# Instance normalisation over 512 channels: from 32 units of 16 channels to 22 units of 16 or 24

## The chip, the cores and the metric

The kernel runs on one core of one Trainium2 chip. The metric is the device time in microseconds (us); the time before is the median of three runs. Engines are called PE (TensorE, matrix products), DVE (VectorE), ACT (ScalarE), POOL (GpSimd) and SP (SyncE, which here only issues transfers). SP, ACT and POOL each have a queue on which they issue transfers (DMA) between the chip's main memory and the on-chip memory of 128 partitions; all queues feed the core's 16 DMA engines.

## What is computed

```python
def setup_inputs():
    B, G, C_per_g, H, W = 4, 8, 16, 256, 256
    return {
        "x": np.random.randn(B, G, C_per_g, H, W).astype(np.float32),
        "gamma": np.random.randn(G, C_per_g).astype(np.float32),
    }

def reference(x, gamma):
    B, G, C_per_g, H, W = x.shape
    mu = x.mean(axis=(3, 4), keepdims=True)
    var = ((x - mu) ** 2).mean(axis=(3, 4), keepdims=True)
    x_norm = (x - mu) / np.sqrt(var + 1e-5)
    out = x_norm * gamma[None, :, :, None, None]
    return out.astype(np.float32)
```

There are 4 x 8 x 16 = 512 channels of 65,536 fp32 values, 256 KB each: 134.2 MB are read and 134.2 MB are written. Each channel is brought to mean 0 and variance 1 and multiplied by its gamma. A channel must be read whole before any of it can be written.

## The kernel before

The input is cut into 32 units of 16 channels, 4 MB each. A channel lies on 8 partitions of a tile of 128 x 8,192 values, so a row of a partition is 32 KB, contiguous in main memory. Six such tiles, the slots `xt0` to `xt5`, take 192 KB of each partition. Unit u lives in slot u mod 6.

The order of the work is written out by hand (the schedule is manual; waits are set by what reads and writes the same tile). Before the loop, POOL issues a small store (`touch`, 16 pieces of 512 bytes of the first output unit, overwritten later) and the load of gamma; then the loads of units 0 to 5 are issued, 1 and 3 on ACT's queue and the others on SP's. POOL builds a mask `navg` of 128 x 128 that holds -1/65536 where two partitions belong to the same channel. Gamma is spread to one value a partition by eight small products of PE (`g_col`, one column for each of the eight units after which gamma repeats).

For each unit, in this order:

- DVE sums each row (`st`, L106), and beside it ACT squares each row and sums the squares (L107; the squares themselves go to `junk`).
- PE multiplies `navg` with the two sums (L115): each partition then has minus its channel's mean and minus its mean square in `ps`.
- DVE makes minus the variance (L116), ACT the root (L120), DVE its reciprocal (L124) and the scale with gamma (L126).
- DVE applies both in one pass over the tile, in place (L135). In unit 0 alone ACT does the last three eighths (L132, with a `shift` that DVE makes, L131).
- ACT issues the store (L139), and SP the load of unit u + 6 into the same slot (L48), which waits for the store to have landed.

Of the kernel before, what the change touches and what calls it, by code (L numbers as in the profile page):

```python
# [1 line left out]

# [4 lines left out]

F32 = mybir.dt.float32
U8 = mybir.dt.uint8
ALU = mybir.AluOpType  # L10
ACTF = mybir.ActivationFunctionType
AX = mybir.AxisListType


@with_exitstack
def kernel(
    ctx: ExitStack,
    tc: tile.TileContext,
    x: bass.AP,
    gamma: bass.AP,  # L20
    out: bass.AP,
):
    nc = tc.nc
    B, G, C, H, W = x.shape
    P = nc.NUM_PARTITIONS
    HW = H * W
    n_ch = B * G * C
    S = 8
    K = P // S
    F = HW // S  # L30
    U = n_ch // K
    NG = (G * C) // K
    AHEAD = 6
    assert HW % S == 0 and (G * C) % K == 0

    xv = x.rearrange("b g c h w -> (b g c h w)").rearrange("(u p f) -> u p f", p=P, f=F)
    ov = out.rearrange("b g c h w -> (b g c h w)").rearrange("(u p f) -> u p f", p=P, f=F)
    gv = gamma.rearrange("g c -> (g c)")

    data = ctx.enter_context(tc.tile_pool(name="data", bufs=1))  # L40
    singles = ctx.enter_context(tc.tile_pool(name="singles", bufs=1))
    psum = ctx.enter_context(tc.tile_pool(name="psum", bufs=4, space=bass.MemoryType.PSUM))
    ctx.enter_context(tc.manual_schedule())

    slots = [data.tile([P, F], F32, name=f"xt{i}") for i in range(AHEAD)]

    def load(u, queue):
        queue.dma_start(out=slots[u % AHEAD][:], in_=xv[u])  # L48


    g_row = singles.tile([1, G * C], F32, name="g_row")
    touch = singles.tile([16, 128], F32, name="touch")
    nc.vector.memset(touch[:], 0.0)  # L53
    nc.gpsimd.dma_start(out=ov[0][0::S, 0:128], in_=touch[:])  # L54
    nc.gpsimd.dma_start(out=g_row[:], in_=gv[None, :])  # L55
    for u in range(AHEAD):
        load(u, nc.scalar if u in (1, 3) else nc.sync)

    eps_t = singles.tile([P, 1], F32, name="eps_t")
    nc.gpsimd.memset(eps_t[:], 1e-5)  # L60
    one = singles.tile([1, 1], F32, name="one")
    nc.gpsimd.memset(one[:], 1.0)
    navg = singles.tile([P, K, S], F32, name="navg")
    nc.gpsimd.memset(navg[:], -1.0 / HW)  # L64
    nc.gpsimd.affine_select(  # L65
        out=navg[:], in_=navg[:], pattern=[[-S, K], [0, S]], compare_op=ALU.is_ge,
        fill=0.0, base=0, channel_multiplier=1,
    )
    nc.gpsimd.affine_select(  # L69
        out=navg[:], in_=navg[:], pattern=[[S, K], [0, S]], compare_op=ALU.is_ge,  # L70
        fill=0.0, base=S - 1, channel_multiplier=-1,
    )
    navg_w = navg[:].rearrange("p k s -> p (k s)")
    root_eps = singles.tile([P, 1], F32, name="root_eps")
    nc.scalar.activation(out=root_eps[:], in_=eps_t[:], func=ACTF.Sqrt)  # L75
    g_rep = singles.tile([1, NG, K, S], F32, name="g_rep")
    g_ps = psum.tile([P, NG], F32, name="g_ps", bufs=1)
    g_col = singles.tile([P, NG], F32, name="g_col")

    nc.vector.tensor_copy(  # L80
        out=g_rep[:],
        in_=g_row[:].rearrange("o (n k) -> o n k", n=NG).unsqueeze(3).to_broadcast([1, NG, K, S]),
    )
    for n in range(NG):
        nc.tensor.matmul(  # L85
            out=g_ps[:, n : n + 1],
            lhsT=g_rep[:, n].rearrange("o k s -> o (k s)"),
            rhs=one[:],
            start=True, stop=True,
        )  # L90
    nc.vector.tensor_copy(out=g_col[:], in_=g_ps[:])  # L91

    junk = singles.tile([P, F], U8, name="junk")

    st = singles.tile([P, U, 2], F32, name="st")
    nvar = singles.tile([P, U], F32, name="nvar")
    std = singles.tile([P, U], F32, name="std")
    rstd = singles.tile([P, U], F32, name="rstd")
    scale = singles.tile([P, U], F32, name="scale")

    shift = singles.tile([P, 1], F32, name="shift")

    squares = []
    for u in range(U):
        t = slots[u % AHEAD]
        nc.vector.reduce_sum(out=st[:, u, 0:1], in_=t[:], axis=AX.X)  # L106
        square = nc.scalar.activation(  # L107
            out=junk[:], in_=t[:], func=ACTF.Square, accum_out=st[:, u, 1:2],
        )
        if u:  # L110

            tc.declare_no_dep(square.ins, squares[-1].ins, reason="junk, ordered by the root between")
        squares.append(square)
        ps = psum.tile([P, 2], F32, name="ps")
        nc.tensor.matmul(out=ps[:], lhsT=navg_w, rhs=st[:, u], start=True, stop=True)  # L115
        nc.vector.tensor_scalar(  # L116
            out=nvar[:, u : u + 1], in0=ps[:, 0:1], scalar1=ps[:, 0:1],
            scalar2=ps[:, 1:2], op0=ALU.mult, op1=ALU.add,
        )
        nc.scalar.activation(  # L120
            out=std[:, u : u + 1], in_=nvar[:, u : u + 1], func=ACTF.Sqrt,
            bias=eps_t[:], scale=-1.0,
        )
        nc.vector.reciprocal(out=rstd[:, u : u + 1], in_=std[:, u : u + 1])  # L124
        g = u % NG
        nc.vector.tensor_mul(  # L126
            out=scale[:, u : u + 1], in0=rstd[:, u : u + 1], in1=g_col[:, g : g + 1],
        )
        cut = F * 5 // 8 if u == 0 else F
        if cut < F:  # L130
            nc.vector.tensor_mul(out=shift[:], in0=ps[:, 0:1], in1=scale[:, u : u + 1])  # L131
            nc.scalar.activation(  # L132
                out=t[:, cut:], in_=t[:, cut:], func=ACTF.Identity, bias=shift[:], scale=scale[:, u : u + 1],
            )
        nc.vector.tensor_scalar(  # L135
            out=t[:, :cut], in0=t[:, :cut], scalar1=ps[:, 0:1], scalar2=scale[:, u : u + 1],
            op0=ALU.add, op1=ALU.mult,
        )
        nc.scalar.dma_start(out=ov[u], in_=t[:])  # L139
        if u + AHEAD < U:  # L140
            load(u + AHEAD, nc.sync)


# [1 line left out]
_INS = ['x', 'gamma']  # L145
_OUTS = [((4, 8, 16, 256, 256), 'float32')]


# [23 lines left out]
```

## Time and profile before

| What | us |
|---|---|
| Time before, median of three runs (627.28 to 627.58) | 627.53 |
| Span of the profiled execution, first to last instruction | 625.2 |
| Time before less that span | 2.3 |
| DVE busy | 441.8 |
| ACT busy | 241.8 |
| One sum of 128 x 8,192 on DVE (L106) | 8.68 |
| One square of 128 x 8,192 on ACT (L107) | 7.03 |
| One apply of 128 x 8,192 on DVE (L135) | 4.55 |
| Store, issue to landing, median | 62.5 |
| Load on SP's queue, issue to landing, median | 38.5 |

The profile is of one execution, and durations are read from it. The runs' times are taken without the profiler: the 2.3 us are the difference of that median and this span, and no time of the profiled execution itself is given beyond its span. In the page, rows of slices cut the span in 40 equal parts; busy shares are in tenths and GB/s is what the DMA engines moved. A group's line gives the line of the kernel, engine, operation, tiles and shapes, the count, the busy time and the mean of one in ns, and the idle time ahead with what ended it. A window's line gives the busy time of each engine between two times of the span.

### The profile page before, as it was taken

What the parts mean: (1) busy time and instruction counts of PE and PEld (TensorE: products, weight loads), DVE (VectorE), ACT (ScalarE), POOL (GpSimd) and SP (SyncE); (2) the same over time, 40 slices, a digit from 0 to 9 for tenths busy, and PEclk for the clock granted to TensorE, in tenths of its full rate; (3) what the DMA queues carried; (4) which work ended last, traced back from release to release, by engine and by line L of the source; (5) the groups of instructions that cost most, each with busy time, mean ns of one, the idle gap of its engine ahead of it and who ended that gap; (6) DMA issues with size and microseconds to landing.
All of it is one profiled execution on the core that took longest, in us unless ns stands there. A gap on an engine that the chain in (4) does not pass through costs nothing.

```text
span 625.2 us, 635 instructions
## 1 busy us (share of the span) xinstructions
PE 21.4 (3%) x80; PEld 19.5 (3%) x80; DVE 441.8 (71%) x164; ACT 241.8 (39%) x99; POOL 2.4 (0%) x11
## 2 busy tenths in 40 slices
PE   0200000000000000000000000000000000000000
PEld 0200000000000000000000000000000000000000
DVE  0589999998776687666786767867668676687730
ACT  0464444444443244432344423444224442244400
POOL 1000000000000000000000000000000000000000
DMA  8999999999999999999999999999999999999998
GB/s 370 436 407 432 436 436 436 436 436 430 423 436 434 434 428 434 434 436 436 436 436 428 426 436 436 432 430 434 434 436 436 436 436 421 432 436 434 434 430 367
DMA packets 9282, 268.46 MB, mean 429 GB/s; under 512 B 1072, under 2 KB 1088, under 8 KB 1088
## 3 DMA queue, kind: packets, MB, share of 16 engines
q10 hardware_dynamic: 4896, 142.61, 52.9%
q1 hardware_dynamic: 4320, 125.83, 46.8%
q0 software_dynamic: 64, 0.01, 0.0%
q14 instruction: 2, 0.02, 0.0%
HBM read 134.22 MB, written 134.23 MB: 429 GB/s over the span
## 4 chain that ended last, share of the span: by engine, by line
another core or an unknown queue 61%; DMA 17%; DVE 15%; SPq 1%; PE 1%; issue 0%; ACT 0%
DMA xt<-in_x_dram 10%; DVE st L106 10%; DMA out_dram<-xt 8%; DVE xt L135 5%; SPq L48 1%; PE ps L115 1%; ACT std L120 0%; DVE nvar L116 0%; DVE rstd L124 0%; DVE scale L126 0%; DVE shift L131 0%
## 5 line engine op out<-in xcount | busy, mean ns | idle before, releaser
L106 DVE TENSOR_REDUCE st<-xt 128x1 f32<-128x8192 f32 x32 | 277.9, 8684 | 102.2 <-DMA xt<-in_x_dram 102.2
L107 ACT ACTIVATE junk<-xt 128x8192 uint8<-128x8192 f32 x32 | 225.0, 7030 | 272.0 <-DMA xt<-in_x_dram 233.8
L135 DVE TENSOR_SCALAR xt<-xt,ps,scale 128x8192 f32<-128x8192 f32 (+1 forms) x32 | 144.0, 4500 | 1.1
L120 ACT ACTIVATE std<-nvar,eps_t 128x1 f32<-128x1 f32 x32 | 9.4, 295 | 79.4 <-DVE nvar L116 79.4
L115 PE MATMUL ps<-st,navg 128*128 128x2 f32 x64 | 17.8, 348 | 557.3 <-DVE st L106 557.3
L115 PEld LDWEIGHTS ps<-st,navg 128*128 128x128 f32 x64 | 16.0, 310 | 559.1 <-issue 546.2
L116 DVE TENSOR_SCALAR nvar<-ps 128x1 f32<-128x1 f32 x32 | 9.2, 286 | 23.8 <-PE ps L115 23.8
L124 DVE RECIPROCAL rstd<-std 128x1 f32<-128x1 f32 x32 | 5.2, 163 | 11.6 <-ACT std L120 11.6
L80 DVE COPY g_rep<-g_row 1x1024 f32<-1x1024 f32 x1 | 0.7, 681 | 14.4 <-DMA g_row<-in_gamma_dram 14.4
L107 ACT ACTIVATION_READ_ACCUMULATOR junk<-xt 128x1 f32 x32 | 6.0, 186 | 0.0
L126 DVE TENSOR_TENSOR scale<-rstd,g_col 128x1 f32<-128x1 f32 x32 | 5.1, 158 | 1.1
L85 PE MATMUL g_ps<-one,g_rep 1*128 1x1 f32 x16 | 3.5, 347 | 16.3 <-DVE g_rep L80 16.3
L85 PEld LDWEIGHTS g_ps<-one,g_rep 1*128 1x128 f32 x16 | 3.5, 326 | 16.3 <-issue 16.3
L132 ACT ACTIVATE xt<-xt,shift,scale 128x3072 f32<-128x3072 f32 x1 | 2.9, 2947 | 0.7 <-DVE shift L131 0.7
L91 DVE COPY g_col<-g_ps 128x8 f32<-128x8 f32 x1 | 0.2, 167 | 3.7 <-PE g_ps L85 3.7
L75 ACT ACT_TABLE_LOAD x1 | 1.3, 1283 | 1.7 <-PEq L156 1.7
L53 DVE MEMSET touch<- 16x128 f32 x1 | 0.2, 165 | 0.9 <-PEq L156 0.9
L54 POOL DMA_DIRECT2D out_dram<-touch x1 | 0.6, 617 | 0.8 <-DVE touch L53 0.8
L55 POOL DMA_DIRECT2D g_row<-in_gamma_dram x1 | 0.5, 487 | 0.0
L65 POOL TENSOR_SCALAR_AFFINE_SELECT navg<-navg 128x128 f32<-128x128 f32 x1 | 0.4, 400 | 0.1
L69 POOL TENSOR_SCALAR_AFFINE_SELECT navg<-navg 128x128 f32<-128x128 f32 x1 | 0.4, 399 | 0.1
L64 POOL MEMSET navg<- 128x128 f32 x1 | 0.2, 230 | 0.0
(8 smaller groups left out, 1.0 us busy)
## 6 DMA issues: line engine op xcount, KB each, us to landing
out_dram<-xt ACTq DMA_DIRECT2D x32, 4096.0 KB, 62.5
xt<-in_x_dram SPq DMA_DIRECT2D x30, 4096.0 KB, 38.5
xt<-in_x_dram ACTq DMA_DIRECT2D x2, 4096.0 KB, 31.7
out_dram<-touch POOLq DMA_DIRECT2D x1, 8.0 KB, 9.3
g_row<-in_gamma_dram POOLq DMA_DIRECT2D x1, 0.5 KB, 13.5
```

The source lines that it names most:

```text
L48: queue.dma_start(out=slots[u % AHEAD][:], in_=xv[u])
L75: nc.scalar.activation(out=root_eps[:], in_=eps_t[:], func=ACTF.Sqrt)
L85: nc.tensor.matmul(out=g_ps[:, n : n + 1], lhsT=g_rep[:, n].rearrange("o k s -> o (k s)"), rhs=one[:], start=True, stop=True,)
L106: nc.vector.reduce_sum(out=st[:, u, 0:1], in_=t[:], axis=AX.X)
L107: square = nc.scalar.activation(out=junk[:], in_=t[:], func=ACTF.Square, accum_out=st[:, u, 1:2],)
L115: nc.tensor.matmul(out=ps[:], lhsT=navg_w, rhs=st[:, u], start=True, stop=True)
L116: nc.vector.tensor_scalar(out=nvar[:, u : u + 1], in0=ps[:, 0:1], scalar1=ps[:, 0:1], scalar2=ps[:, 1:2], op0=ALU.mult, op1=ALU.add,)
L120: nc.scalar.activation(out=std[:, u : u + 1], in_=nvar[:, u : u + 1], func=ACTF.Sqrt, bias=eps_t[:], scale=-1.0,)
L124: nc.vector.reciprocal(out=rstd[:, u : u + 1], in_=std[:, u : u + 1])
L126: nc.vector.tensor_mul(out=scale[:, u : u + 1], in0=rstd[:, u : u + 1], in1=g_col[:, g : g + 1],)
L132: nc.scalar.activation(out=t[:, cut:], in_=t[:, cut:], func=ACTF.Identity, bias=shift[:], scale=scale[:, u : u + 1],)
L135: nc.vector.tensor_scalar(out=t[:, :cut], in0=t[:, :cut], scalar1=ps[:, 0:1], scalar2=scale[:, u : u + 1], op0=ALU.add, op1=ALU.mult,)
```

## The change

The units become larger and fewer: one of 16 channels (4 MB) at each end and 20 of 24 channels (6 MB) between them, 22 in all. In a unit of 24 channels a row of a partition is three pieces of 4,096 values, 48 KB; a channel is 16 pieces and so lies on 5 and a third partitions. There are four slots of 48 KB a partition instead of six of 32 KB. Unit u + 4 is loaded into the slot of unit u.

All loads are issued on SP's queue, but for the first third of the rows of unit 1, which goes on ACT's.

In a unit of 24 channels DVE sums each of the three pieces of a row in one instruction, and ACT squares them in three. Every partition holds pieces of at most two channels, at places that repeat every 8 partitions. A mask `by_c` sorts the three pieces' sums to three columns, by channel (a product and a sum on DVE), one product of PE over groups of 16 partitions adds them up, and the mask `by_j` sorts the results back to the pieces (again a product and a sum). The variance then takes two DVE instructions instead of one, on three values a partition; root, reciprocal and scale also hold three values. The apply is three instructions of 4,096 values. In units 0, 1, 2 and the last, ACT applies part of the tile: a third in units of 24 channels, three eighths in those of 16.

POOL builds five masks instead of one. Gamma is spread to all partitions by one product of PE and sorted to the pieces by 16 small DVE instructions.

The diff's core:

```diff
-    S = 8
-    K = P // S
-    F = HW // S
-    U = n_ch // K
-    NG = (G * C) // K
-    AHEAD = 6
+    F = 4096
+    SLOTS = 4
+    sizes = [2] * 1 + [3] * ((n_ch - 16 * 2) // 24) + [2] * 1
+    U = len(sizes)
+    starts = [sum(sizes[:i]) for i in range(U)]
+    split = {1: 1}
+    helped = (0, 1, 2, U - 1)
...
-    slots = [data.tile([P, F], F32, name=f"xt{i}") for i in range(AHEAD)]
-    def load(u, queue):
-        queue.dma_start(out=slots[u % AHEAD][:], in_=xv[u])
+    slots = [data.tile([P, 3 * F], F32, name=f"xt{i}") for i in range(SLOTS)]
+    def load(u):
+        cut = split.get(u, 0) * F
+        if cut:
+            nc.scalar.dma_start(out=home(u)[:, :cut], in_=rows(xf, u)[:, :cut])
+        if cut < sizes[u] * F:
+            nc.sync.dma_start(out=home(u)[:, cut:], in_=rows(xf, u)[:, cut:])
...
-    for u in range(AHEAD):
-        load(u, nc.scalar if u in (1, 3) else nc.sync)
+    for u in range(SLOTS):
+        load(u)
...
+    g_ps = psum.tile([P, GC], F32, name="g_ps", bufs=1)
+    nc.tensor.matmul(out=g_ps[:], lhsT=ones[:], rhs=g_row[:], start=True, stop=True)
+    g_all = singles.tile([P, GC + 32], F32, name="g_all")
+    nc.vector.tensor_copy(out=g_all[:, :GC], in_=g_ps[:])
+    nc.vector.tensor_copy(out=g_all[:, GC:], in_=g_ps[:, :32])
+    g_ch = singles.tile([P, GC // 8, 3], F32, name="g_ch")
+    for b in range(8):
+        near = g_all[:, 3 * b : 3 * b + GC].rearrange("p (m k) -> p m k", k=8)[:, :, :3]
...
     for u in range(U):
+        t = home(u)
+        three = sizes[u] == 3
+        n = sizes[u] if three else 1
+        step = sizes[u] * F // n
+        nc.vector.reduce_sum(
+            out=st[:, u, :n, 0], in_=t.rearrange("p (j f) -> p j f", j=n), axis=AX.X,
+        )
+        for j in range(n):
+            square = nc.scalar.activation(
+                out=junk[:, :step], in_=t[:, j * step : (j + 1) * step],
+                func=ACTF.Square, accum_out=st[:, u, j, 1:2],
+            )
...
+        if three:
+            nc.vector.tensor_mul(
+                out=parts[:],
+                in0=st[:, u].rearrange("p j v -> p v j").unsqueeze(1).to_broadcast([P, 3, 2, 3]),
+                in1=by_c[:].unsqueeze(2).to_broadcast([P, 3, 2, 3]),
+            )
+            nc.vector.reduce_sum(out=sums[:, u], in_=parts[:], axis=AX.X)
+            nc.tensor.matmul(
+                out=ps[:], lhsT=navg3, rhs=sums[:, u].rearrange("p k v -> p (k v)"),
+                start=True, stop=True,
+            )
+            nc.vector.tensor_mul(
+                out=picks[:],
+                in0=ps[:].rearrange("p (k v) -> p v k", v=2).unsqueeze(1).to_broadcast([P, 3, 2, 3]),
+                in1=by_j[:].unsqueeze(2).to_broadcast([P, 3, 2, 3]),
+            )
+            nc.vector.reduce_sum(out=means[:, u], in_=picks[:], axis=AX.X)
+            mean = means[:, u, :, 0]
+            nc.vector.tensor_mul(out=nvar[:, u], in0=mean, in1=mean)
+            nc.vector.tensor_add(out=nvar[:, u], in0=nvar[:, u], in1=means[:, u, :, 1])
...
+        cut = sizes[u] * F
+        if u in helped:
+            cut = 2 * F if three else cut * 5 // 8
...
+        for j in range(n):
+            lo, hi = j * step, min((j + 1) * step, cut)
+            if lo < hi:
+                nc.vector.tensor_scalar(
+                    out=t[:, lo:hi], in0=t[:, lo:hi], scalar1=mean[:, j : j + 1],
+                    scalar2=scale[:, u, j : j + 1], op0=ALU.add, op1=ALU.mult,
+                )
+        nc.scalar.dma_start(out=rows(of, u), in_=t)
+        if u + SLOTS < U:
+            load(u + SLOTS)
```

## The prediction

> **What bounds the kernel now.** I read the page first, for the engine shares and the transfer rate in 40 slices, then the queues.
>
> ```profile
> span 625.2 us, 635 instructions
> PE 21.4 (3%) x80; PEld 19.5 (3%) x80; DVE 441.8 (71%) x164; ACT 241.8 (39%) x99; POOL 2.4 (0%) x11
> DMA  8999999999999999999999999999999999999998
> GB/s 370 436 407 432 436 436 436 436 436 430 423 436 434 434 428 434 434 436 436 436 436 428 426 436 436 432 430 434 434 436 436 436 436 421 432 436 434 434 430 367
> ...
> q10 hardware_dynamic: 4896, 142.61, 52.9%
> q1 hardware_dynamic: 4320, 125.83, 46.8%
> ```
>
> The DMA row is at 9 in all slices but the first and the last: the transfer engines never rest, while VectorE (DVE) is busy 71% of the span. 268.4 MB must move whatever the tiling, so only three things can shorten the span: what one transfer costs beyond its bytes, the stretches below the steady rate, and the ends. The windows give the second (last column GB/s, the one before it the DMA share):
>
> ```profile
> core 0: us, PE busy (x) PEld busy (x) DVE busy (x) ACT busy (x) POOL busy (x), PEclk, DMA share, GB/s
> 36.50:60.00 23.50, 0.63 (x3) 0.61 (x3) 22.10 (x6) 14.54 (x5) 0.00 (x0) 1.00 1.00 417
> 160.27:585.60 425.33, 12.26 (x44) 11.01 (x44) 304.07 (x111) 162.68 (x67) 0.00 (x0) 1.00 1.00 433
> 600.62:625.20 24.58, 0.00 (x0) 0.00 (x0) 0.00 (x0) 0.00 (x0) 0.00 (x0) 1.00 0.89 385
> ```
>
> The rate is 433 GB/s while loads and stores run side by side. In the stretch in which the first store begins it is 417: 23.5 us x 16/433 = 0.9 us lost once. Even after the last instruction of VectorE the transfers run on: the last store is issued at 600.62 and begins only when three earlier ones are out. The timeline's end shows that cover:
>
> ```profile
> 585.57 8.69 DVE L106 TENSOR_REDUCE st<-xt 128x1 f32<-128x8192 f32 x1 [4.33 <-DMA xt<-in_x_dram]
> 596.03 4.55 DVE L135 TENSOR_SCALAR xt<-xt,ps,scale 128x8192 f32<-128x8192 f32 x1
> 600.62 0.34 ACTq L139 DMA_DIRECT2D out_dram<-xt  x1
> ```
>
> The trace's records of single DMA packets give the first and the third. A 32 KB row is one packet; an engine takes one from SyncE's queue (q1) and one from ScalarE's (q10) in turn, and starts the next 1,209 ns after the last (16 of them and two completion packets make the 19.36 us in which 8 MB pass). A transfer ends with a 4-byte completion packet on each engine, after which the next starts 6 ns later. First packet at 1.82 us; the first ones take up to 1.94 us for 1.21, so some 0.7 us of read latency; last packet's end 623.9, then 1.3 us to the end of the span. Per engine: 512 x 1.209 + 64 x 0.006 = 619.4, + 1.8 + 0.7 + 0.9 + 1.3 = 624.1; the other 1.1 is the spread of the engines (the last ends 1.0 us after the first). The time shown outside the profile is 627.53, 2.3 us over this span; I carry the 2.3 over unchanged.
>
> **Part by part. Fewer packets and transfers** (on the path). Per engine each transfer has 8 rows. After: 39 transfers of 48 KB rows (312 packets), 5 of 32 KB (40), one of 16 KB (8): 360 packets for 512, and 45 completions for 64. What a packet costs beyond its bytes lies between 0 and the 6 ns that a completion packet with its 4 bytes takes; I take 5. So 152 x 5 = 0.76 us, and 19 x 6 = 0.11 us: 0.9 us less, between 0.1 and 1.0. The Trainium skill (DMA: Bandwidth & Descriptors, Why small descriptors are slow) gives about 3 cycles of overhead a packet; by its 850 MHz that is 3.5 ns, an estimate by which this term would be 0.65.
>
> **VectorE's and ScalarE's work on a unit** (beside the transfers). These rows price it:
>
> ```profile
> L106 DVE TENSOR_REDUCE st<-xt 128x1 f32<-128x8192 f32 x32 | 277.9, 8684 | 102.2 <-DMA xt<-in_x_dram 102.2
> L116 DVE TENSOR_SCALAR nvar<-ps 128x1 f32<-128x1 f32 x32 | 9.2, 286 | 23.8 <-PE ps L115 23.8
> L126 DVE TENSOR_TENSOR scale<-rstd,g_col 128x1 f32<-128x1 f32 x32 | 5.1, 158 | 1.1
> L135 DVE TENSOR_SCALAR xt<-xt,ps,scale 128x5120 f32<-128x5120 f32 x1 | 2.9, 2941 | 0.0
> ```
>
> Sum over 12,288 elements: 8.68 x 1.5 = 13.0 us. Apply: 4.55 us for 8,192 and 2.94 for 5,120 elements make 0.52 ns an element and 0.26 us fixed, so three of 4,096 take 3 x 2.40 = 7.2. The chain between them now takes 1.8 us; added are the products and sums with the two masks (parts, sums, picks, means) and one more step for the variance, 5 instructions of 0.16 to 0.29 us and their gaps: 0.9 to 1.7, taken 1.2, so 3.0. Together 23.2 us a unit, against 1.5 x 19.36 = 29.0 us that its 12 MB need on the engines (now 15.1 of 19.4). ScalarE: 7,030 ns for 8,192 elements and 2,947 for 3,072 (L132) make 0.80 ns an element, so a square of 4,096 takes 3.8 and its read-out 0.19: 12 us for three, less than the sum beside it. PE still makes one product a unit, of 6 columns for 2, some 0.6 us either way. All this costs nothing as long as both queues have something to do.
>
> **The start** (beside the transfers). Loads 0 to 3 are all on SyncE's queue but for a third of unit 1. Unit 0 takes turns with that third: 2.5 + 8 x (1.21 + 0.60) = 17.0 us, where now units 0 and 1 land together at 22.4. Gamma is set up ahead of it on VectorE: gamma lands at 15.5 now, two queues' packets at a time ahead of it; with a 16 KB packet among them 13 to 15.5. Behind it stand a product of PE and 16 small instructions of 0.16 to 0.29 us, some 4 us: the sum of unit 0 begins between 17.5 and 20, taken 19. GpSimd's 12 added fills and selects (0.1 to 0.4 us each, some 3 us in all) are done by 7 us. Store 0 follows after 8.7 + 1.9 + 2.9 + 0.3 us at 33, its first packet at 34 (a transfer's first packet comes 1.0 us after its issue, as at the start). Until then loads alone run, which would last until 55.7: no gap. Without that cover every microsecond would count.
>
> **Four slots for six** (beside the transfers). By 34 us load 2 (from 26.7, 1.81 a packet) has sent 4 of its 8 packets. From there each engine takes one packet of each queue in turn, and as every transfer has 8, each store ends when a load is half through. Load u+4 on SyncE waits for store u; it is issued while load u+3 has 4 rounds of 3.62 = 14.5 us to go, and needs some 2.7 (1.3 to report, 0.4 to issue, 1.0 to start): 11.8 us to spare. Nothing else is queued on SyncE behind that wait. Store u is issued 23.9 us after its load lands and is due 14.5 us after the next one's landing, 43.5: 19.6 to spare. Store 1 is ready at 33 + 13.0 + 3.0 + 4.8 = 54 and due at 58.
>
> **The end** (on the path if late). When load 21 lands, stores 19 (half), 20 and 21 are left: 7.2 + 14.5 + 9.7 = 31.4 us before 623.0, so at 591.6. Unit 21 then needs 0.4 + 8.7 + 1.9 + 2.9 + 0.3 = 14.2: ready at 605.8, due at 613.3, 7.5 to spare (now 13.6). Store 20, ready about 591, is due at 598.8. No loss.
>
> **Sum.** 625.2 - 0.9 = 624.3 of span, + 2.3 = 626.6.
>
> **Rivals.** (1) The loss at the first store goes too. Its 0.9 us fell where the second load of both queues ended and the first store entered behind one of them (the slow packets lie between 39.9 and 43.3 us); now q10 is empty when store 0 comes. For: no later end of transfers shows such a loss. Against: it is the first large write in either kernel. 626.6 - 0.9 = 625.7.
>
> (2) Slower: loads on one queue show their read latency. Between 17 and 34 us SyncE's queue is alone, 12 packets an engine, which the trace never has with loads (the first four came on two queues). Bounds: 0, from stores alone at the end (a packet each 1,209 ns), and the 0.7 us of the first packets: 12 x 0.7 = 8.4 us, 635.0. From 0.18 us a packet on it decides (12 x 0.18 = 0.9 + 1.25). Against: a packet starts before the one ahead ends, so reads go ahead. I take 0.
>
> (3) A 48 KB row is not one packet. Cut in three of 16 KB there are 936 + 48 = 984 packets an engine: 472 x 5 ns - 0.1 = 2.3 us more than now, 629.8. No row of the trace is over 32 KB; nothing else speaks for it. This is the case in which the change doesn't do what it says.
>
> (4) Compute runs the tail dry: a unit would have to take over 7.5 us more, a third more than priced; each further microsecond adds one, some 630 with 3 us.
>
> (5) Fewer transfers save their fixed cost: 1.3 us from last packet to report, 19 times, 24.7 us: 601.9. Against: transfers overlap; stores alone at the end finish 9.68 us apart, which is 8 packets and 6 ns. The Trainium skill (DMA: Bandwidth & Descriptors, Anatomy of one DMA) fits a transfer as 2.0 us plus its bytes, an estimate of 38 us for 19; by these 9.68 us that is latency, not engine time.
>
> **How the numbers follow.** A measurement of this kernel tells about 0.2%, 1.25 us: faster is under 626.3, slower over 628.8. Chances: forecast 0.50, rival 1 0.29, 2 0.08, 3 0.07, 4 0.05, 5 0.01. Of the forecast some 0.08 lies under 626.3 (less spread of the engines, up to 1.0 us in this execution): faster 0.29 + 0.01 + 0.08 = 0.38, slower 0.08 + 0.07 + 0.05 = 0.20, same 0.42. Range: from rival 1 with half of the spread gone, 625.2, to rival 3 and most of rival 4, 630.0; outside lie rivals 2, 5 and part of 1 and 4, under 0.2.
>
> **What would show it.** Right: DMA packets fall from 9,282 to about 6,600, the steady stretch rises by about 0.5 GB/s, the DMA row stays at 9, the last store is issued near 606 and its packets begin near 613, SyncE still waits on stores. Rival 1: no dip of the GB/s row near 34 us. Rival 2: a dip between 17 and 34 us. Rival 3: some 16,500 packets. Rival 4: slices under 9 near the end, and VectorE's last instructions after 613. Wrong altogether if a slice in the middle falls under 9.

## Result and the profile after

Over 21 runs of each kernel on the same chips the changed kernel takes 628.30 us (627.11 to 630.84) and the one before 627.00 (626.66 to 627.59): a ratio of 1.0020, interval [1.0015, 1.0026]. It is slower by 1.3 us, where the forecast had it 0.9 faster, and its runs spread over 3.7 us instead of 0.9. The execution profiled below took 627.52, 1.7 more than its span.

Its page, from the span to the queues:

```profile
span 625.8 us, 717 instructions
...
PE 13.2 (2%) x46; PEld 11.5 (2%) x46; DVE 451.7 (72%) x271; ACT 258.3 (41%) x152; POOL 5.1 (1%) x23
...
DMA  9999999999999999999999999999999999999997
GB/s 382 440 392 433 449 440 415 449 440 418 450 418 434 446 415 443 443 418 446 434 427 443 421 437 447 415 446 440 418 446 424 434 449 412 446 443 422 441 424 325
DMA packets 6549, 268.48 MB, mean 429 GB/s; under 512 B 769, under 2 KB 785, under 8 KB 785
...
q10 hardware_dynamic: 3312, 136.32, 50.3%
q1 hardware_dynamic: 3168, 132.12, 49.0%
q14 instruction: 5, 0.03, 0.0%
```

The DMA row is at 9 to the last slice but one, and packets fell to 6,549. What is worse than before is above all the last slice, 325 GB/s for 367. The slices between swing by up to 38 GB/s only because a slice of 15.6 us holds eight or nine packets of 1.81 us. The windows show where the end goes (last columns DMA share and GB/s; a packet counts in the window in which it begins):

```profile
36.50:60.00 23.50, 0.56 (x2) 0.50 (x2) 22.08 (x13) 18.38 (x11) 0.00 (x0) 1.00 1.03 446
160.27:585.60 425.33, 8.48 (x30) 7.54 (x30) 314.37 (x178) 171.37 (x105) 0.00 (x0) 1.00 1.00 434
600.62:625.20 24.58, 0.56 (x2) 0.50 (x2) 5.02 (x6) 3.24 (x2) 0.00 (x0) 1.00 0.86 373
622.00:623.00 1.00, 0.00 (x0) 0.00 (x0) 0.00 (x0) 0.00 (x0) 0.00 (x0) 1.00 0.16 66
623.00:624.00 1.00, 0.00 (x0) 0.00 (x0) 0.00 (x0) 0.00 (x0) 0.00 (x0) 1.00 0.08 33
```

The same last two windows of the kernel before:

```profile
622.00:623.00 1.00, 0.00 (x0) 0.00 (x0) 0.00 (x0) 0.00 (x0) 0.00 (x0) 1.00 0.84 360
623.00:624.00 1.00, 0.00 (x0) 0.00 (x0) 0.00 (x0) 0.00 (x0) 0.00 (x0) 1.00 0.01 0
```

One 32 KB packet is 33 GB/s and a share of 0.08 in such a window. Between 622 and 623 us only two packets begin in the changed kernel, for eleven before: most engines are done earlier. Then a single engine goes on past 624. By the trace's records of single packets, put together to the chains of the 16 engines (a packet begins where the one ahead on its engine ends), the first engine ends at 622.05 (before 622.91) and the last at 624.39 (before 623.93). The engine that ends last has from 60 us on the same 316 data packets as the others whose chain can be followed that far: no engine takes over work of a late one, so the last one sets the end.

What makes an engine late shows in the same records, in two kinds. The first is q14, the instruction code on its way to the compute engines, in packets of 8 KB. The page of before has two:

```profile
q14 instruction: 2, 0.02, 0.0%
```

Both fell into the run, one of them on the engine that ends last. Now there are four (the fifth in the page has 32 bytes), two of them on the engine that ends last. Each takes 0.31 us of its engine and makes the next packet longer: by 0.54 us each on that engine, 1.7 us there in all, and by 0.11 and 0.15 on the engine that has the other two. The second kind is slow packets: between 60 and 570 us, over some 0.06 us longer than usual, with no code packet just ahead. The change has ten, of 48 KB, 0.07 to 0.51 us longer than 1.81 (before: five, of at most 0.15).

The engines' work came out as priced. From the groups and the timeline of the changed kernel:

```profile
L178 DVE TENSOR_REDUCE st<-xt 128x3 f32<-128x12288 f32 x20 | 259.1, 12952 | 109.2 <-DMA xt<-in_x_dram 109.2
L182 ACT ACTIVATE junk<-xt 128x4096 uint8<-128x4096 f32 x60 | 217.0, 3617 | 240.4 <-DMA xt<-in_x_dram 237.5 <-DVE xt L238 1.2 <-ACT xt L231 0.4
```

```profile
569.03 12.95 DVE L178 TENSOR_REDUCE st<-xt 128x3 f32<-128x12288 f32 x1 [6.20 <-DMA xt<-in_x_dram]
...
584.77 7.06 DVE L238 TENSOR_SCALAR xt<-xt,means,scale 128x4096 f32<-128x4096 f32 x3
591.87 0.34 ACTq L242 DMA_DIRECT2D out_dram<-xt  x1
...
593.32 8.69 DVE L178 TENSOR_REDUCE st<-xt 128x1 f32<-128x8192 f32 x1 [1.49 <-DMA xt<-in_x_dram]
...
607.01 0.34 ACTq L242 DMA_DIRECT2D out_dram<-xt  x1
```

VectorE and ScalarE wait for loads (last columns), the chain between sum and apply is 2.8 us, the last store is issued at 607.0 and its first packets begin between 612.4 and 613.7, behind the store ahead.

### The profile page after: what moved, and what is told of

The parts are those of the page before. It is cut to its first block, busy times and chain, and to the rows that moved or that the text cites. A ratio compares the mean times of both kernels' runs of the same rounds, so it can differ in the third digit from the quotient of the medians.

```text
span 625.8 us, 717 instructions
## 1 busy us (share of the span) xinstructions
PE 13.2 (2%) x46; PEld 11.5 (2%) x46; DVE 451.7 (72%) x271; ACT 258.3 (41%) x152; POOL 5.1 (1%) x23
## 2 busy tenths in 40 slices
DMA packets 6549, 268.48 MB, mean 429 GB/s; under 512 B 769, under 2 KB 785, under 8 KB 785
## 4 chain that ended last, share of the span: by engine, by line
DMA 71%; DVE 24%; PE 1%; ACT 1%; issue 1%; DVEq 0%; ACTq 0%; SPq 0%
DMA xt<-in_x_dram 65%; DVE st L178 21%; DMA out_dram<-xt 6%; DVE xt L238 1%; PE ps L197 1%; ACT xt L231 0%; DVE parts L191 0%; DVE picks L201 0%; DVE sums L196 0%; PE ps L212 0%; DVE means L206 0%; ACT std L220 0%; DVE nvar L214 0%; DVE rstd L223 0%; DVE scale L224 0%
## 5 line engine op out<-in xcount | busy, mean ns | idle before, releaser
L178 DVE TENSOR_REDUCE st<-xt 128x3 f32<-128x12288 f32 (+1 forms) x22 | 276.4, 12565 | 111.2 <-DMA xt<-in_x_dram 111.2
L182 ACT ACTIVATE junk<-xt 128x4096 uint8<-128x4096 f32 (+1 forms) x62 | 231.1, 3727 | 264.5 <-DMA xt<-in_x_dram 261.6
L238 DVE TENSOR_SCALAR xt<-xt,means,scale 128x4096 f32<-128x4096 f32 x58 | 136.5, 2408 | 0.7
L220 ACT ACTIVATE std<-nvar,eps_t 128x3 f32<-128x3 f32 (+1 forms) x22 | 6.5, 297 | 80.1 <-DVE nvar L209 74.8
L197 PE MATMUL ps<-sums,navg 128*128 128x6 f32 x40 | 11.4, 356 | 544.5 <-DVE sums L196 544.5
L197 PEld LDWEIGHTS ps<-sums,navg 128*128 128x128 f32 x40 | 10.0, 312 | 545.8 <-issue 503.8
L231 ACT ACTIVATE xt<-xt,shift,scale 128x3072 f32<-128x3072 f32 (+1 forms) x4 | 13.5, 3374 | 2.8 <-DVE shift L228 2.8
L182 ACT ACTIVATION_READ_ACCUMULATOR junk<-xt 128x1 f32 x62 | 11.6, 186 | 0.0
L238 DVE TENSOR_SCALAR xt<-xt,ps,scale 128x5120 f32<-128x5120 f32 x2 | 5.9, 2942 | 0.0
L212 PE MATMUL ps<-st,navg 128*128 128x2 f32 x4 | 1.1, 348 | 32.4 <-DVE st L178 32.4
```

Source lines behind the costliest of these rows:

```text
L178: nc.vector.reduce_sum(out=st[:, u, :n, 0], in_=t.rearrange("p (j f) -> p j f", j=n), axis=AX.X,)
L182: square = nc.scalar.activation(out=junk[:, :step], in_=t[:, j * step : (j + 1) * step], func=ACTF.Square, accum_out=st[:, u, j, 1:2],)
L197: nc.tensor.matmul(out=ps[:], lhsT=navg3, rhs=sums[:, u].rearrange("p k v -> p (k v)"), start=True, stop=True,)
L220: nc.scalar.activation(out=std[:, u, :n], in_=nvar[:, u, :n], func=ACTF.Sqrt, bias=eps_t[:], scale=-1.0,)
L231: nc.scalar.activation(out=t[:, cut:], in_=t[:, cut:], func=ACTF.Identity, bias=shift[:, u : u + 1], scale=scale[:, u, n - 1 : n],)
L238: nc.vector.tensor_scalar(out=t[:, lo:hi], in0=t[:, lo:hi], scalar1=mean[:, j : j + 1], scalar2=scale[:, u, j : j + 1], op0=ALU.add, op1=A ...
```

## The experiments

The expectations use letters. A: the longer program's instruction code. B: loads and stores whose beginnings do not fall together. C: the 48 KB rows. D: how far apart in main memory the two streams are. L: the length of a packet. P: the pitch of rows (48 KB; P2: 64 KB). F: beginnings one packet apart. "Late" is an engine's delay against its packets' usual times. Every experiment shares its chip with runs of the kernel before.

**The changed kernel again, its code removed, and code added to the kernel before.** The first is the change as it is. The second keeps the 48 KB rows and leaves out the assignment of pieces to channels (a row counts as one piece, and its statistics are those of 16 rows):

```diff
-        n = sizes[u] if three else 1
+        n = 1
...
-        if three:
-            nc.vector.tensor_mul(out=parts[:], ...)
...
+        nc.tensor.matmul(out=ps[:, :2], lhsT=navg3 if three else navg2, rhs=st[:, u, 0], start=True, stop=True)
```

The third is the kernel before with 12 small copies more a unit:

```diff
         nc.scalar.dma_start(out=ov[u], in_=t[:])
+        if u < U - 1:
+            for i in range(12):
+                nc.vector.tensor_copy(out=idle[:, i : i + 1], in_=scale[:, u : u + 1])
```

> The changed kernel as it is, for a second trace. All theories hold that each of the 16 DMA engines has 0.9 us less to do than before, and that the time is set by the engine that is latest. Theory A (instruction code): 8 KB instruction packets on queue q14 appear in the middle of the run, 4 of them (2 before), each makes one engine 0.5 to 0.9 us late, and they fall on the same two engines as in the first trace. Theory B (boundaries): most of the lateness comes from other slow packets, which stand beside a transfer's beginning, since loads and stores no longer begin together. Theory C (rows): slow packets of 48 KB come anywhere. Time: 627 to 630 us.

> The changed kernel's transfers unchanged (48 KB rows, four slots, the same queues), but a row counts as one piece: one sum, one square, one apply, no sorting. It leaves out the assignment of pieces to channels (statistics are those of 16 rows). VectorE has some 120 instructions, ScalarE some 100, PE some 90. Theory A: no instruction packet in the middle of the run, the latest engine is 0.5 to 1 us behind the earliest, 625.5 to 626.3 us, faster than before by 1 us. Theory B and C: still slow packets at the beginnings or anywhere, 627.5 to 628.5 us, slower than before.

> The kernel before with 12 more small copies of one value a partition on VectorE after each unit but the last (372 instructions, 2 us a unit, beside the transfers). Theory A: three more instruction packets on q14 in the middle of the run, on the engine that already has one, each 0.8 us: that engine ends 2.5 us later, 628.8 to 629.6 us. Theory B and C: no change, 627.0 us, since transfers, rows and boundaries are those of before.

The change again: 630.72 (627.96 to 634.23), ratio 1.0057 [1.0034, 1.0079]; its profile is of the longest run:

```profile
span 632.5 us, 717 instructions
...
GB/s 382 431 414 448 441 405 445 448 417 429 448 441 404 448 445 432 417 441 445 407 441 448 432 410 448 438 420 432 445 441 407 445 445 426 423 425 444 392 419 213
...
q14 instruction: 4, 0.03, 0.0%
```

```profile
624.00:625.00 1.00, 0.00 (x0) 0.00 (x0) 0.00 (x0) 0.00 (x0) 0.00 (x0) 1.00 0.08 33
625.00:626.00 1.00, 0.00 (x0) 0.00 (x0) 0.00 (x0) 0.00 (x0) 0.00 (x0) 1.00 0.15 66
...
628.00:629.00 1.00, 0.00 (x0) 0.00 (x0) 0.00 (x0) 0.00 (x0) 0.00 (x0) 1.00 0.08 33
```

There are four code packets of 8 KB, as in the run of 625.8 us; the slow packets are 45 for 10, up to 0.82 us longer than usual. One or two engines work alone from 624 to 631. The late engine also made the last load land late: the last sum begins at 600.03, for 593.32 in the first profile, and the last store is issued at 613.7. That eats the 6 us by which it was early (607.0 to 613): the last two stores came late, and the first engine ends 2.3 us later than in the first profile.

Without the sorting: 629.87 (628.06 to 632.49), ratio 1.0045 [1.0027, 1.0062].

```profile
span 626.9 us, 455 instructions
...
PE 13.0 (2%) x46; PEld 11.5 (2%) x46; DVE 425.7 (68%) x116; ACT 246.4 (39%) x72; POOL 3.3 (1%) x14
...
q14 instruction: 2, 0.02, 0.0%
```

The code is back to two packets, with 116 instructions on VectorE for 271, and the time is no better and as wide: 20 slow packets, the last engine at 625.4. No code packet is on that engine: its 2.7 us of delay are packets that took longer than usual. So code alone is not the cause.

With more code in the kernel before: 629.50 (629.29 to 629.59), ratio 1.0039 [1.0026, 1.0052].

```profile
span 627.6 us, 1007 instructions
...
PE 21.4 (3%) x80; PEld 19.5 (3%) x80; DVE 464.4 (74%) x536; ACT 241.8 (39%) x99; POOL 2.4 (0%) x11
...
q14 instruction: 5, 0.04, 0.0%
```

```profile
622.00:623.00 1.00, 0.00 (x0) 0.00 (x0) 0.00 (x0) 0.00 (x0) 0.00 (x0) 1.00 0.53 229
623.00:624.00 1.00, 0.00 (x0) 0.00 (x0) 0.00 (x0) 0.00 (x0) 0.00 (x0) 1.00 0.08 33
...
625.00:626.00 1.00, 0.00 (x0) 0.00 (x0) 0.00 (x0) 0.00 (x0) 0.00 (x0) 1.00 0.08 33
```

VectorE's own time does not matter (74% busy). One DMA engine is 3.5 us late; it works all but alone from 623 to 626.3, and the time rises by 2.4 us. Two of the five code packets can be followed in the records to that engine. That four fall on it is worked out: after 60 us no packet of this run is more than 0.14 us longer than usual except behind a code packet, and four code packets with what they add to the next one (0.53 to 0.61 us) make 3.5. That is cause A by itself, and it gives a narrow spread. The Trainium skill (Runtime: NRT & Kernel Launch, Instruction fetch mechanics) has engines refill instructions in blocks of 16 KiB by a DMA whose cost is "mostly hidden". Here the packets are of 8 KB, and in a kernel that its DMA engines bind each costs the DMA engine that carries it 0.4 to 0.9 us (0.31 and 0.11 to 0.61 on the next packet): the measurement decides.

**Beginnings together or not.** Two kernels: the changed one with loads 1 and 3 whole on ScalarE's queue, and the kernel before with three quarters of unit 1 there and all else on SyncE's, so that its stores begin five or six packets after a load.

```diff
-    split = {1: 1}
+    split = {1: 3, 3: 3}
```

```diff
-        queue.dma_start(out=slots[u % AHEAD][:], in_=xv[u])
+        cut = F * 3 // 4 if u == 1 else 0
+        if cut:
+            nc.scalar.dma_start(out=slots[u][:, :cut], in_=xv[u][:, :cut])
+        queue.dma_start(out=slots[u % AHEAD][:, cut:], in_=xv[u][:, cut:])
...
-        load(u, nc.scalar if u in (1, 3) else nc.sync)
+        load(u, nc.sync)
...
-        cut = F * 5 // 8 if u == 0 else F
+        cut = F
```

> The changed kernel with loads 1 and 3 whole on ScalarE's queue, as before, so that loads and stores again begin together on both queues. Theory B: the slow packets at the beginnings go, 626.0 to 627.0 us. Theory A: the 4 instruction packets stay, 627.0 to 629 us, like the changed kernel. Theory C: like the changed kernel.

> The kernel before with another start alone: three quarters of unit 1's rows on ScalarE's queue, all other loads on SyncE's, and unit 0 applied whole by VectorE. So store 0 should begin three or four packets into a load, and stores and loads should no longer begin together, with 32 KB rows and the same instructions as before. Theory B (boundaries): slow load packets appear beside the beginnings of transfers, the engines drift apart by 2 to 5 us, 628 to 631 us, with a wide spread of runs. Theory C (48 KB rows): no change, 626.5 to 627.5 us. Theory A (instruction code alone): no change.

The first took 630.35 (628.15 to 631.87) with 43 slow packets, but its stores still began five or six packets after one load and two or three ahead of the next (a transfer has eight an engine), so it did not test what it was made for. The second took 627.73 (627.29 to 628.04), ratio 1.0012 [1.0003, 1.0021], without one slow packet. Its profiled span is 0.64 us longer than that of before. Of this, 0.2 lie ahead of the last packet's end (around the first store an engine loses 1.0 us on average, for 0.8) and the rest behind it (1.75 us for 1.30), which no run explains. So with 32 KB rows these beginnings make no packet slow, while the first kernel, with nearly the same beginnings, has 43 slow packets of 48 KB. What was left for B was 48 KB rows whose beginnings fall together:

```diff
-    split = {1: 1}
+    split = {3: (3072, 5120)}
...
+        cut = 0
+        for end in split.get(u, ()):
+            nc.scalar.dma_start(out=home(u)[:, cut:end], in_=rows(xf, u)[:, cut:end])
+            cut = end
```

This deals part of unit 3 to ScalarE's queue in two pieces, after which each load begins with a store. A twin has the same edit in the kernel without sorting.

> The changed kernel with another start: of its loads only two pieces of unit 3 (12 KB and 8 KB of each row) go on ScalarE's queue, at the very start, sized so that store 0, store 1 and store 2 each begin when a load begins. Loads and stores then change over together, with 48 KB rows; e4 did not reach this (its stores began two packets from the loads). Theory B: hardly any slow packets beside the beginnings; the four instruction packets stay, two on one engine: 626.5 to 627.5 us, a narrow spread. Theory C: as the changed kernel, 628 to 632 us.

> e2 (a row as one piece, sorting of pieces to channels left out) with the start of e6. Theory A and B together: no or few instruction packets and no slow packets at the beginnings, engines within 1 us of each other: 625.3 to 626.3 us, 1 us faster than before. Theory C: 628 to 632 us as e2.

They took 719.75 (719.02 to 721.18), ratio 1.148 [1.1466, 1.1497], and 724.03. Neither theory had that. The page of the first and a window of its middle:

```profile
span 719.5 us, 719 instructions
...
DMA  9999999999999999999999999999999999999996
GB/s 376 421 430 399 337 386 366 369 369 380 375 372 377 372 372 355 377 374 374 363 383 363 374 385 369 377 369 380 374 377 374 363 380 372 385 367 374 337 391 288
```

```profile
160.27:585.60 425.33, 7.33 (x26) 6.51 (x26) 271.72 (x156) 144.35 (x89) 0.00 (x0) 1.00 0.99 373
```

The share is 0.99 and the rate 373 for 434: the engines do not wait, each packet takes longer. A 48 KB packet takes 2.1 us on average for 1.81, up to 4.1, loads and stores alike, on all engines. Over half of these packets are slow, for ten in the change. The kernel before, whose loads and stores also begin together, has five slow packets of 32 KB.

**Distance or length.** Two more kernels put the streams elsewhere by taking the units in another order: the one just shown with 6 MB between loads and stores instead of 12, and the kernel before with 12 MB. A third is the change in the first one's order. The fourth cuts every transfer in two half rows, 24 KB a packet.

```diff
+    mixed = [0] + [k for i in range(1, 11) for k in (i, i + 10)] + [21]
+    starts = [starts[k] for k in mixed]
```

```diff
+    far = [24, 27, 30, 25, 28, 31, 26, 29]
+    turn = [k for i in range(8) for k in (3 * i, 3 * i + 1, 3 * i + 2, far[i])]
```

```diff
-            nc.sync.dma_start(out=home(u)[:, cut:], in_=rows(xf, u)[:, cut:])
+            mid = (cut + sizes[u] * F) // 2
+            nc.sync.dma_start(out=home(u)[:, cut:mid], in_=rows(xf, u)[:, cut:mid])
+            nc.sync.dma_start(out=home(u)[:, mid:], in_=rows(xf, u)[:, mid:])
...
-        nc.scalar.dma_start(out=rows(of, u), in_=t)
+        mid = sizes[u] * F // 2
+        nc.scalar.dma_start(out=rows(of, u)[:, :mid], in_=t[:, :mid])
+        nc.scalar.dma_start(out=rows(of, u)[:, mid:], in_=t[:, mid:])
```

> e6 took 720 us: its 48 KB packets, of loads and stores alike, on all engines and at all places, took 2.1 us for 1.81. In e6 a load and the store beside it are always exactly 12 MB apart in their tensors (row r of unit u + 2 with row r of unit u). Theory D (main memory): it is this distance of the two streams that collides, rows of 48 KB or not. Here the units of 24 channels are taken in the order 1, 11, 2, 12, ..., so that the streams are 6 MB apart; slots, queues, start and rows are those of e6. Theory D: another time by many us, near 627 to 632 if 6 MB does not collide. Theory C (48 KB rows at the same place in their slots, whatever the addresses): 715 to 725 us.

> The kernel before (32 KB rows, load and store 16 MB apart) with its units in another order, so that load and store are 12 MB apart for three quarters of the units. Theory D, if the distance alone matters: slower by tens of us, towards 700. Theory C: 627 us as before.

> The changed kernel with the unit order of e8. Stores begin halfway a load as in the changed kernel, so the distance is 6 MB less four rows, or 60 MB less and more in turn, instead of 12 MB and 18 MB by four rows. Theory D: the slow packets at the beginnings of transfers change in number, the time moves by more than its spread, to 626.5 to 627.5 us or to over 632. Theory A alone or C: 627 to 631 us, like the changed kernel.

> e6 (720 us) with every load and store of the loop cut into two transfers of half rows, so that packets are 24 KB; the rows still lie 48 KB apart in main memory, and loads and stores still begin together. Theory L (length of a packet: an engine that alternates 48 KB of load and 48 KB of store gets slow): back to 626 to 629 us. Theory P (the distance of 48 KB between the rows that the engines work on at a time): 700 us or more, as e6.

The distance is not it: 723.69 at 6 MB for 719.75 at 12, and the kernel before at 12 MB took 626.89, ratio 1.0000 [0.9991, 1.0009]. The change in the other order took 630.72 (628.21 to 633.96) with 47 slow packets, as the change itself did when it was run again. The half rows brought the 720 us back to 629.49 (629.37 to 629.65):

```profile
span 627.8 us, 839 instructions
...
DMA packets 13029, 268.49 MB, mean 428 GB/s; under 512 B 1488, under 2 KB 1504, under 8 KB 1504
```

No slow packet is left, at the same pitch. The beginnings are not the same, though: by the records a store's transfers now mostly begin three or four packets into a load's, and not with it, so this run alone does not tell length from beginnings. The same cut in the change itself, and in the kernel without sorting:

> The changed kernel with every transfer but the first third of unit 1 cut into two of half rows (24 or 16 KB packets). By the fixed cost of a packet and a completion every engine has 1.9 us more to do than in the changed kernel. Theory L with A: hardly a slow packet beside the instruction packets, which stay (5 or 6 of them, at least two on one engine); 628.5 to 629.5 us with a spread of runs under 0.7 us. If length is not the cause at this start: 630 to 634 us with a spread of 3 us or more.

> e2 (sorting of pieces to channels left out, 628 to 632 us) cut in the same way. Theory L with A: two instruction packets on two engines, no other slow packets, 627.3 to 628.3 us with a spread under 0.7 us, so 1.1 us less than e13 (the sorting's instruction packets). If length is not the cause: 629 to 633 us, a spread of 3 us or more.

The change with half rows: 629.33 (629.18 to 629.52), ratio 1.0036 [1.0024, 1.0049].

```profile
span 627.4 us, 837 instructions
...
DMA packets 12885, 268.49 MB, mean 428 GB/s; under 512 B 1472, under 2 KB 1488, under 8 KB 1488
...
q14 instruction: 5, 0.04, 0.0%
```

```profile
622.00:623.00 1.00, 0.00 (x0) 0.00 (x0) 0.00 (x0) 0.00 (x0) 0.00 (x0) 1.00 1.15 492
623.00:624.00 1.00, 0.00 (x0) 0.00 (x0) 0.00 (x0) 0.00 (x0) 0.00 (x0) 1.00 0.81 344
```

Here about half of the stores' transfers begin with a load's, as in the kernel of 720 us, and the others one packet later, and at most one slow packet is left: it is the length of the packet. All engines are now at work to 623.8: the first ends 1.8 us later than in the change, where twice the packets and transfers were to cost 1.9. The spread of runs falls from 3.7 to 0.3 us with the slow packets. The last engine is the one with two code packets (0.31 and 0.53 to 0.54 us each), as in the change. So the change without slow packets would take some 629.3 - 1.8 = 627.5, an estimate. Without the sorting and in half rows it is 628.55 (628.31 to 629.61), ratio 1.0025 [1.0016, 1.0035], above its expectation (627.3 to 628.3). Its records show a third code packet, but not on which engine it fell, so the difference stays open.

**64 KB rows, and 32 KB packets in them.** Fifteen units of 32 channels, one of 16 at each end, three slots; then the same with each transfer in halves.

```diff
-    F = 4096
-    SLOTS = 4
+    F = 8192
+    SLOTS = 3
...
-    sizes = [2] * 1 + [3] * ((n_ch - 16 * 2) // 24) + [2] * 1
+    sizes = [1] + [2] * 15 + [1]
```

> A version of its own that keeps the whole computation: 15 units of 32 channels in 64 KB rows (4 rows a channel, no sorting) in three slots, and a unit of 16 channels in 32 KB rows at each end; about 110 instructions on VectorE, 100 on ScalarE, 70 on PE. Theory A: no instruction packets, or one; by the packets' fixed cost 1.4 us less engine time than before. Theory P: rows 64 KB apart behave as rows 32 KB apart do, no slow packets: 624.5 to 626 us, faster than before by 1 to 2 us. Theory L: packets of 64 KB, slow packets more than in the changed kernel, 628 to 720 us; if the rows are cut into packets of 32 KB, 626 us.

> e12 (units of 32 channels in 64 KB rows, whole computation) with each unit loaded and stored as two transfers of half rows, so packets of 32 KB as before, and applied in two instructions. Theory L with A: packets, completions and instruction packets are those of before, so 626.3 to 627.3 us, the same as before, with a narrow spread. If the rows' distance matters: over 629 us.

Whole: 634.09 (632.41 to 635.03), ratio 1.0112 [1.0095, 1.0128], and 77 slow packets; but this window shows something else as well:

```profile
583.00:599.00 16.00, 0.56 (x2) 0.50 (x2) 14.82 (x7) 2.57 (x3) 0.00 (x0) 1.00 0.72 301
```

The engines rest for a quarter of these 16 us, since unit 15 is ready late (VectorE at 14.82 of 16): 16 x (433 - 301)/433 = 4.9 us, most of the 5.5 us by which the profiled run (632.41) is longer than before. In halves: 635.24 (631.01 to 642.68), where 626.3 to 627.3 was expected. The profile is of a run of 631.23:

```profile
622.00:624.00 2.00, 0.00 (x0) 0.00 (x0) 0.00 (x0) 0.00 (x0) 0.00 (x0) 1.00 0.61 262
624.00:627.00 3.00, 0.00 (x0) 0.00 (x0) 0.00 (x0) 0.00 (x0) 0.00 (x0) 1.00 0.08 33
```

One engine runs alone again, to 628.0. It holds 17 of the 20 slow packets of the run, nearly all where a store began one packet after a load, and no code packet; they and smaller delays make it 4.7 us late. So 32 KB packets can be slow too, and length is not the whole of it. Theory F was then tried on the kernel before, its loads set as in the second kernel of "beginnings", the first store to be moved a few microseconds by work on ScalarE ahead of it: first a square to `junk`, then a copy of half of the tile in place, for which the store has to wait.

```diff
+        if u == 0:
+            late = nc.scalar.activation(out=junk[:, :4096], in_=t[:, 4096:], func=ACTF.Square)
```

```diff
+        if u == 0:
+            nc.scalar.activation(out=t[:, 4096:], in_=t[:, 4096:], func=ACTF.Identity)
```

> e5 (the kernel before with another start) with one more square of 4,096 values on ScalarE ahead of the first store, 3.6 us, so that stores begin one packet after a load instead of five. Rows of 32 KB, 32 KB apart. Theory F (the beginnings one packet apart are what makes late engines later): slow load packets at stores' beginnings, over 628.5 us, a spread of 2 us or more. Theory P2 (rows 64 KB apart): no slow packets beside the two instruction packets, 627 to 628.2 us, a narrow spread, as e5.

> e16 with the added work on ScalarE in the stored tile itself (half of unit 0 copied onto itself, 3.8 us), so that the first store must wait for it and stores begin about one packet after a load. Theory F (beginnings one packet apart): slow load packets at stores' beginnings, over 628.5 us, a spread of 2 us or more. Theory P2 (rows 64 KB apart): no slow packets beside the two instruction packets, 627 to 628.5 us, a spread under 1 us.

The square did not move the store, which went out while it ran: 627.68 (627.48 to 629.04), so it does not bear on F. The copy moved it, but to where beginnings coincide as in the kernel before, so F was not tested. Of its five runs the profiled one is the shortest (627.80; 622.9 and 624.3 us for the first and the last engine, four slow packets); the others took 629.5 to 630.6, and no profile shows why.

## Why the prediction failed

**Right: the fixed costs.** The first engine ends 0.86 us earlier, for 0.9. A 24 KB packet starts every 908 ns and a 48 KB one every 1,811: 2 x 908 - 1,811 = 5 ns a packet, the value taken. Sum, apply, chain and square (13.0, 7.1, 2.8 and 3.6 us) were priced within 0.2, the last stores within 1.2 us, and in the profiled execution their cover held. Rivals 2, 3 and 5 did not come: 438 GB/s from 17 to 34 us, 6,549 packets, no transfer cost regained. Nor did rival 1: at 34 us, just ahead of the first store's packets, sixteen load packets still took 2.5 to 2.7 us for 1.81, some 0.8 us lost. Rival 4 came only as a follower, in the run of 634.2 us, behind a late engine. Two readings were a little off, without weight in the sum: the slowest of the first packets took 2.01 us and not 1.94, and the first store's packets began at 36.6 us and not at 34, though it was issued at 31.7 and not 33.

**The step that failed: "the other 1.1 is the spread of the engines".** It was carried over as a constant, and where it was allowed to move it shrank, toward faster. The end is the last engine's end; a gain that all engines share counts only if no engine becomes later. In the profiled executions the spread went from 1.02 to 2.34 us: -0.86 + 1.32 + 0.11 behind the last packet is the +0.57 of the two spans. Of the 1.32, some 0.85 is one code packet more on the last engine (1.7 for 0.85), 0.39 is packets on it that took longer than usual, and 0.09 was there at 60 us. The median run lies 0.8 above the profiled one. That this too is slow packets is not seen in that run and so is not shown; for it speaks that half rows come out at some 627.5, with hardly any spread, once their fixed cost is taken off. That 628.30 still lies inside the range of 625.2 to 630.0 is luck: the upper part of the range stood for rivals 3 and 4, which are not what made the kernel slower. Run again, the change took 630.72, which lies outside.

So two terms were missing. The instruction code stood in the page of before (q14, two packets) and was not priced, although the change takes VectorE from 164 to 271 instructions. And a 48 KB packet was taken as 1.5 packets of 32 KB, since "no row of the trace is over 32 KB": that bound was asked about its number of packets, not about its time. Half rows show the difference: with packets of 24 KB the runs spread over 0.3 us for 3.7. A third, smaller: the 2.3 us around the span mixed one execution's span with other runs' median. The changed kernel's own profiled run shows 1.7, so the sum was 0.6 high, which hid part of the miss.

**Open.** Why a long packet becomes slow, why half of them do when loads and stores begin together, and why 32 KB packets in 64 KB rows put nearly all of the delay on one engine. The distance between the two streams hardly matters at the two values tried (6 and 12 MB). Beginnings do not make packets of 24 KB slow in 48 KB rows, nor packets of 32 KB in 32 KB rows by more than 0.15 us; at 48 KB a packet they decide how many are slow. No version here beat the kernel before.

## What to carry to other kernels

Where DMA engines never rest, price what makes the last engine late, not only what all engines save: each code packet (q14, about one more for every 107 to 133 instructions added on VectorE here: 164, 271 and 536 instructions gave one, two and, as worked out above, four on the engine that ended last) is worth 0.85 us there. Longer rows save 5 ns a packet and can lose a hundred times that in one slow packet; run a longer packet by itself, several times, before building a tiling on it. A fraction of a microsecond from a profile needs that execution's own time, and a spread of runs that widens is itself a finding.

## What was not expected of the hardware

- 48 KB packets: one every 1,811 ns in most cases; when loads and stores begin together 2.1 us on average and 720 us in all; with 24 KB packets no such slowness (629.3).
- Instruction code shares the DMA engines: 0.31 us for 8 KB and 0.11 to 0.61 on the next packet, two of four on the engine that ended last.
- Around the first store every engine loses time once, 0.8 us on average before, 0.8 after and 1.0 in the kernel before with other beginnings, with the loads on one queue or two.
